# Two transformer blocks on one Trainium2 core: another ordering model, loose ends dealt among products, gate rows in one pass

## The chip, the cores and the metric

The kernel runs on one core of one Trainium2 chip, as one program. The metric is the time of one execution on the device in microseconds. The kernel before has a median of 2524.74 us over three runs (2521.05 to 2525.29).

## The reference, cut to what matters

A sequence of 512 tokens of width 1024 goes through two blocks, all in float32.

```python
# first block
h = rms_norm(x, norm1_g); proj = h @ w_in                # q, k, v and three conv branches
y_attn = chunked_relpos_attention(q, k, v, ...)          # 16 heads, chunks of 64, relative bias
y_conv = bg * conv_w3(cg * xc)                           # gated short convolution
gates = sigmoid(h @ w_gate + b_gate)                     # two branches
x = x + (g_attn * (y_attn @ w_attn_proj) + g_conv * (y_conv @ w_conv_proj)) @ w_out
h2 = rms_norm(x, norm2_g)
x = x + square(relu(h2 @ w_up)) @ w_down                 # 1024 -> 4096 -> 1024
# second block
mod = silu(c) @ w_ada + b_ada                            # six shift, scale and gate vectors
h = rms_norm(x, g_norm1) * (1 + scale1) + shift1
proj = h @ w_in_2
y_sb = stick_breaking(q_sb, k_sb, v_sb)                  # 8 heads of 64, normalised after
y_ml = mlstm(q_ml, k_ml, v_ml, i_pre, f_pre)             # 4 heads of 128; i and f are 4 columns each
x = x + gate1 * (concat(y_sb, y_ml) @ w_out)
h2 = rms_norm(x, g_norm2) * (1 + scale2) + shift2
x = x + gate2 * peer(h2)       # 8 heads: top 16 of 128 x 128 keys, 16384 experts of one row each
```

In `mlstm` the forget gates are summed over time (`A`), the input gates less `A` get a running maximum (`grow`), and each head needs its row of these over all 128 partitions.

## The kernel before, in words

Activations lie transposed, as eight tiles of 128 features x 512 tokens. A value is kept as two parts in a reduced format of float32 that TensorE takes in one pass: a rounded high part and the rest as a low part. A product of weights and activations is three such passes (`mm3`, lines 152 to 156): high by high, high by low, low by high. A weight tile of 1 MB (256 output columns) is loaded by SP into `wraw`, cast on ScalarE into `whi` (line 143) and subtracted on VectorE into `wlo` (line 145), with two buffers of each. `linear` (line 158) makes one 128-row output of 24 passes, `linear2` (line 166) two at once.

**Order.** The program is written as one stream. At the end the framework sets the order of each engine's instructions: it runs the program on a simulated machine and, at each step, gives an engine the earliest instruction of the stream that is ready in that run. The orders are then fixed; on the chip the engines run them in sequence and wait on semaphores. Two simulated machines are to be had; the kernel before uses the default. DMAs are issued in such an order too, nearly all on SP's queue. Tiles come from pools that are opened and closed like a stack, on the left or right side of the memory; a tile that gets memory which another had waits for the last reader of that one.

**First block (`block1`, line 264).** While the inputs load, nine products of ones run (line 285). SP loads the eight x tiles, ScalarE issues the first weight tile in eight pieces of 128 KB (line 289), then makes gain tiles (x times the norm's gain, high and low, `gain_tile`, line 224) and weight halves piece by piece. The gain tiles (pool `hp1`, 32 KB of each partition) are the inputs of all products up to the end of attention, but the pool stays open to the end of the merge. The merge stage makes gates, the attention projection and the output product (lines 403 to 409); behind each of its eight outputs the residual is added and its squares are summed. Then pool `hp2` is opened and all eight gain tiles of the second norm are made (`gain_split`, line 414) before the up product.

**Second block's mixer (`mix`, line 665).** `stick_breaking` (line 821) has two groups of four heads. A head is a generator of seven steps: three of scores, three of shares (cumulative sums by products with a triangle, an exponential, high and low parts) and one that weighs the values. Steps of a head and of the head before it are interleaved ("nonoono", line 913), which leaves four steps of the last head over. At the start of the second group these four run behind the four products that make its queries and keys (lines 899 to 903); at the end four run alone (line 917). `mlstm_in` (line 921) is a generator of the products that feed the mLSTM, each with a short convolution on VectorE and a store; fourteen of its steps follow after `gates` (line 766). `gates` makes the i and f rows by one `linear` whose weight tile has the four i columns at 0 and the four f columns at 32, then their scans, and returns `grow` and `frow` as 4 x 512 tiles of full float32. In `mlstm` (lines 978 and 1020) a product with a selector of ones (`sel`, 4 x 128 for each head) spreads one row over 128 partitions, twice for each head.

**Peer (`peer`, line 1040).** Keys are scored and ranked on VectorE, while products of the first expert weights run ahead (`ahead`). Then one-hot products spread the chosen gates (`spread`), and the experts follow: 128 groups of 128 experts, with weights streamed at 1 MB a tile, while the last 128 tokens are done by gathering rows.

Of the kernel before, what the change touches and what calls it, by code (L numbers as in the profile page):

```python
# [8 lines left out]
F32 = mybir.dt.float32  # L9
F32R = mybir.dt.float32r  # L10
# [11 lines left out]
P = 128  # L22
D = 1024
T = 512
KO = D // P
# [17 lines left out]
V_N1, V_N2, V_GN1, V_GN2 = 0, 8, 16, 24  # L43
# [5 lines left out]
C_ID, C_BONE, C_TRI, C_SBM, C_MLM, C_IOTA, C_SEL, C_ROW = 0, 128, 256, 384, 768, 896, 1024, 1536  # L49
# [20 lines left out]
class Ker:  # L70
# [193 lines left out]
    def block1(self, es_x):  # L264
        from contextlib import ExitStack
        nc, I = self.nc, self.I
# [3 lines left out]
        with ExitStack() as es:  # L270
            hp = es.enter_context(self.pool("hp1", bufs=KO))
            yp = es.enter_context(self.pool("yp1", bufs=KO))
            sp = es.enter_context(self.pool("sp1"))
# [6 lines left out]
            with self.pool("n1") as tp:  # L280
                x0, hs = [], []
                raw, hi, lo = self.weight_tiles()
                pt = self.psum("c", 1)
                for _ in range(9):
                    nc.tensor.matmul(pt[:, :P], self.ones, self.ones, start=True, stop=True)
                for k in range(KO):
                    xt = tp.tile([P, T], F32, name=f"x0_{k}")
                    nc.sync.dma_start(xt, I["x"][k])
                    nc.scalar.dma_start(raw[:, k, :], I["w_in"][16][:, k, :])
                    x0.append(xt)  # L290
                    if k == 0:
                        nc.sync.dma_start(*self.fixed[0])
                nc.sync.dma_start(*self.fixed[1])
                for k, xt in enumerate(x0):
                    hs.append(self.gain_tile(hp, xt, self.v(V_N1 + k), "h1", KO))
                    nc.scalar.copy(hi[:, k, :], raw[:, k, :])  # L296
                    nc.vector.tensor_sub(lo[:, k, :], raw[:, k, :], hi[:, k, :].bitcast(F32))
                nc.vector.tensor_scalar_mul(bgh, self.v(V_BG, 16), 0.5)
                pcs = self.linear2((hi, lo), hs)
                pxs = self.linear2(self.weights(I["w_in"][20]), hs)  # L300
                acc = None
                for k in range(KO):
                    acc = self.sum_sq(tp, acc, x0[k])
                self.rsqrt(tp, self.col_sums(acc), 1.0 / D, out=rstd)
                nc.vector.tensor_mul(rstd2, rstd, rstd)
                pt = self.psum("c", 1)
                for i in range(4):
                    nc.tensor.transpose(pt[:, i * P:(i + 1) * P], rstd[:, i * P:(i + 1) * P], self.ident)
                nc.vector.tensor_copy(rtok, pt.rearrange("p (a b) -> p a b", b=P)[:, :, 0])


            with self.pool("cv", bufs=2) as tp, self.pool("cva") as sp:
                ada = self.ada(sp, range(8))
                ycs = []
                for g in range(4):
# [9 lines left out]
                    for j in range(2):  # L325
                        n = 2 * g + j
# [38 lines left out]
            with self.banks(a=3, b=2, c=2, d=1) as self.ps:  # L365
                ya = self.attention(hs, yp, rstd, rtok, g_dram)

            es_b = es_x.enter_context(ExitStack())
            self.ps = es_b.enter_context(self.banks(a=8))
            with self.pool("mg", bufs=2) as tp, self.pool("mgy", bufs=KO) as mp:  # L370
# [22 lines left out]
                xs = []  # L393
# [4 lines left out]
                for k in range(KO):  # L398
                    xt = xp.tile([P, T], F32, name=f"x{k}")
                    nc.sync.dma_start(xt, I["x"][k])  # L400
                    xs.append(xt)
                acc = None
                for g in range(4):
                    w = self.weights(I["w_out"][g])
                    for j in range(2):
                        n = 2 * g + j
                        po = self.linear(w, j, ms)
                        nc.vector.tensor_add(xs[n], po, xs[n])
                        acc = self.sum_sq(nq, acc, xs[n])
        self.xs = xs  # L410
        self.hp2 = ExitStack()
        hp = self.hp2.enter_context(self.pool("hp2", bufs=KO, side="right"))
        with self.pool("up", bufs=KO + 4) as up, self.pool("mlt", bufs=2) as tp, self.pool("mls") as sp:
            hs = self.gain_split(hp, xs, V_N2, "h2", KO)
            rstd = sp.tile([P, T], F32, name="rstd2")
# [249 lines left out]
    def mix(self, es_x):  # L665
# [21 lines left out]
        with ExitStack() as es:  # L687
# [4 lines left out]
            nc.sync.dma_start(self.mlc, I["consts"][:, C_MLM:C_MLM + P])  # L692
            self.sel = sp.tile([4, 4 * P], F32, name="sel")
            nc.sync.dma_start(self.sel, I["consts"][0:4, C_SEL:C_SEL + 4 * P])
            with self.pool("ci") as tp:
                ci = tp.tile([P, 4 * P], F32, name="ci")
                nc.sync.dma_start(ci, I["consts"][:, C_TRI:C_TRI + 4 * P])
                nc.scalar.copy(cr[:, P:2 * P], ci[:, 0:P])
                nc.scalar.copy(cr[:, 3 * P:6 * P], ci[:, P:4 * P])
            nc.scalar.copy(cr[:, 0:P], self.ident)  # L700
            nc.vector.tensor_scalar_mul(cr[:, 2 * P:3 * P], self.ones, -1.0)
# [6 lines left out]
            steps = lambda n: [next(ml_in, None) for _ in range(n)]  # L708
            mixed = self.stick_breaking(mp, hs, q0, pk)
            rows = self.gates(sp, hs)  # L710
            steps(14)
            es_b.close()
# [53 lines left out]
    def gates(self, sp, hs):  # L766

        nc, I = self.nc, self.I
        with self.pool("gt") as tp:
            raw = tp.tile([P, KO, P], F32, name="if_w")  # L770
            nc.sync.dma_start(raw, I["w_if"])
            hi = tp.tile([P, KO, P], F32R, name="if_h")
            lo = tp.tile([P, KO, P], F32R, name="if_l")
            nc.scalar.copy(hi, raw)
            nc.vector.tensor_sub(lo, raw, hi.bitcast(F32))
            ps = self.linear((hi, lo), 0, hs, tag="b")
            z = tp.tile([P, T], F32, name="if_z")
            nc.scalar.activation(z[:36], ps[:36], AF.Identity, bias=self.v(V_GB)[:36])
            f = tp.tile([4, T], F32, name="if_f")
            nc.vector.tensor_copy(f, z[32:36])  # L780
# [11 lines left out]
            nc.vector.tensor_sub(b, z[0:4], A)  # L792
            grow = sp.tile([4, T], F32, name="grow")
            nc.vector.tensor_tensor_scan(grow, one, b, 0.0, op0=ALU.mult, op1=ALU.max)
            frow = sp.tile([4, T], F32, name="frow")
            nc.vector.tensor_add(frow, A, grow)
# [6 lines left out]
            nc.vector.tensor_copy(bt, pb[:, :16])  # L803
        return bt, grow, frow

# [14 lines left out]

    def stick_breaking(self, mp, hs, pq, pk):
        nc, I = self.nc, self.I
        widths = [512, 384, 256, 256]
        out = []
        with self.pool("sb") as tp, self.pool("sbq", bufs=2) as qp, self.pool("sbv", bufs=4) as vp:
# [70 lines left out]
            for g in range(2):  # L896
                if g:
                    pq, pk = [], []
                    for p, at in ((pq, 0), (pk, 2)):
                        w = self.weights(I["w_in_2"][at + g])  # L900
                        p += [self.qk_in(tp, self.linear(w, j, hs), None) for j in range(2)]
                    for _ in old:
                        pass
                    old = None
                else:
                    pk = [self.qk_in(tp, p, None) for p in pk]
# [3 lines left out]
                for j in range(2):  # L910
                    for f in range(2):
# [4 lines left out]
                        old = new  # L916
            for _ in old:
                pass
        return out
# [638 lines left out]
```

## Time and profile before

| | us |
|---|---|
| median of three runs | 2524.74 |
| the profiled execution | 2522.37 |
| its span, first to last instruction | 2520.6 |
| TensorE busy | 2467.9 (98%) |
| VectorE busy | 1872.7 (74%) |
| ScalarE busy | 1056.6 (42%) |
| GpSimd busy | 624.1 (25%) |
| DMA | 515.03 MB, 204 GB/s over the span |

The profile is of one execution. Busy time counts work, not issuing or waiting; of TensorE the ends of products are modelled. A wait is given to the one that ended it last. The granted clock is a share of the full 2.4 GHz.

### The profile page before, as it was taken

How to read it: one execution, taken by the hardware profiler on the slowest of the kernel's cores; microseconds unless marked ns; L12 is line 12 of the kernel's file. 1: busy time of each engine (PE TensorE's matmuls, PEld its weight loads, DVE VectorE, ACT ScalarE, POOL GpSimd, SP SyncE). 2: the span in 40 equal slices, each digit the busy share in tenths (PEclk: the TensorE clock that was granted, in tenths of full speed). 3: DMA queues.
4: the chain of work that ended last, by engine and by line, in shares of the span. 5: the costliest groups of instructions: out<-in, count | busy, mean ns of one | idle time of the engine just before them, and what ended most of it. 6: DMA issues, size and time to landing. Idle time of an engine off the chain costs nothing.

```text
span 2520.6 us, 33112 instructions
## 1 busy us (share of the span) xinstructions
PE 2467.9 (98%) x12655; PEld 2114.4 (84%) x12655; DVE 1872.7 (74%) x3094; ACT 1056.6 (42%) x1480; POOL 624.1 (25%) x506
## 2 busy tenths in 40 slices
PE   9999999999999999999999989999999999999999
PEld 7887887877888887777789988978889999999998
DVE  5558777855555557897779999857668787888887
ACT  5226555643222236766653345543333333333332
POOL 0001100111011001001035630011135555555552
PEclk9999999999999999999999999999999999999999
DMA  5352323443444332114343357799879999999995
GB/s 202 127 199 99 104 93 101 139 170 135 174 150 148 138 137 85 38 67 138 120 162 120 124 184 276 311 319 341 300 267 333 327 339 333 328 336 335 336 340 195
DMA packets 172312, 515.03 MB, mean 204 GB/s; under 512 B 13396, under 2 KB 78308, under 8 KB 146296
## 3 DMA queue, kind: packets, MB, share of 16 engines
q1 hardware_dynamic: 133960, 376.52, 42.6%
q0 software_dynamic: 37040, 135.35, 14.9%
q8 instruction: 99, 1.62, 0.2%
q10 hardware_dynamic: 1152, 1.05, 0.1%
q14 instruction: 61, 0.50, 0.1%
HBM read 461.47 MB, written 51.38 MB: 203 GB/s over the span
## 4 chain that ended last, share of the span: by engine, by line
PE 76%; DVE 15%; ACT 4%; DMA 2%; issue 2%; SPq 0%; POOL 0%; ACTq 0%; DVEq 0%; POOLq 0%
PE pa L154 12%; PE pa L156 12%; PE pa L155 12%; PE pp L1443 7%; PE pp L1442 7%; PE pp L1446 7%; PE pu L154 4%; PE pu L156 4%; PE pu L155 4%; DVE wlo L145 1%; ACT whi L143 1%; DVE tk_rest L1194 1%; PE pb L596 1%; DVE tk_e L1230 1%; DMA mg_a<-g_dram 1%
## 5 line engine op out<-in xcount | busy, mean ns | idle before, releaser
L143 ACT CAST whi<-wraw 128x2048 fp32r<-128x2048 f32 x229 | 437.6, 1911 | 540.6 <-PE pa L155 296.5
L145 DVE TENSOR_TENSOR wlo<-wraw,whi 128x2048 fp32r<-128x2048 f32 x210 | 489.0, 2329 | 125.7 <-ACT whi L143 119.3
L154 PE MATMUL pa<-hh,whi 128*128 128x512 f32 (+1 forms) x1360 | 523.0, 385 | 7.1 <-ACT whi L296 3.4
L156 PE MATMUL pa<-hh,wlo 128*128 128x512 f32 (+1 forms) x1360 | 516.4, 381 | 2.3 <-DVE wlo L145 2.2
L155 PE MATMUL pa<-lh,whi 128*128 128x512 f32 (+1 forms) x1360 | 518.4, 381 | 0.0
L1443 PE MATMUL pp<-wlo,hew 128*128 128x512 f32 x768 | 299.0, 390 | 1.5 <-DVE wlo L145 1.5
L1442 PE MATMUL pp<-whi,hew 128*128 128x512 f32 x768 | 298.7, 390 | 1.7 <-ACT hew L1409 1.1
L1152 POOL DMA_INDIRECT r_row<-in_u_rows,r_at x128 | 184.4, 1440 | 461.7 <-DVE r_w L1173 419.6
L154 PEld LDWEIGHTS pa<-hh,whi 128*128 128x128 f32 x1360 | 257.6, 190 | 47.0 <-ACT whi L296 3.6
L156 PEld LDWEIGHTS pa<-hh,wlo 128*128 128x128 f32 x1360 | 257.2, 189 | 44.6 <-issue 3.6
L155 PEld LDWEIGHTS pa<-lh,whi 128*128 128x128 f32 x1360 | 257.5, 189 | 40.9 <-issue 5.3
L1446 PE MATMUL pp<-whi,lew 128*128 128x512 f32 x768 | 237.1, 389 | 0.0
L1152 POOL DMA_INDIRECT r_row<-in_expert_v,r_at x128 | 194.0, 1516 | 173.2 <-DVE r_big L1181 135.7
L156 PE MATMUL pu<-hh,wlo 128*128 128x384 f32 x640 | 215.0, 336 | 0.0
L154 PE MATMUL pu<-hh,whi 128*128 128x384 f32 x640 | 215.0, 336 | 0.0
L155 PE MATMUL pu<-lh,whi 128*128 128x384 f32 x640 | 214.9, 336 | 0.0
L1446 PEld LDWEIGHTS pp<-whi,lew 128*128 128x128 f32 x768 | 144.1, 188 | 30.3
L1443 PEld LDWEIGHTS pp<-wlo,hew 128*128 128x128 f32 x768 | 144.1, 188 | 29.6 <-DVE wlo L145 2.3
L1442 PEld LDWEIGHTS pp<-whi,hew 128*128 128x128 f32 x768 | 144.1, 188 | 29.2 <-ACT hew L1409 1.3
L1181 DVE SCALAR_TENSOR_TENSOR r_big<-r_row,r_w,r_big 128x1024 f32<-128x1024 f32 x127 | 162.9, 1283 | 3.0
L1409 ACT CAST hew<-ex_w 128x384 fp32r<-128x384 f32 x128 | 65.5, 513 | 226.3 <-DVE ex_w L1405 149.1
L1173 DVE CUSTOM_DVE_ANT_0 r_row<-r_row,r_big 128x1024 f32<-128x1024 f32 x128 | 151.3, 1220 | 0.0
(440 smaller groups left out, 4480.1 us busy)
## 6 DMA issues: line engine op xcount, KB each, us to landing
wraw<-in_expert_u SPq DMA_DIRECT2D x64, 1024.0 KB, 7.4
wraw<-in_expert_v SPq DMA_DIRECT2D x64, 1024.0 KB, 7.6
wraw<-in_w_in SPq DMA_DIRECT2D x37, 1024.0 KB, 4.9
ada_w<-in_w_ada SPq DMA_DIRECT2D x24, 1024.0 KB, 4.8
gate_dram<-oh_s SPq DMA_DIRECT2D x12, 2048.0 KB, 7.0
ex_g<-gate_dram SPq DMA_DIRECT2D x31, 768.0 KB, 10.9
wraw<-in_w_up SPq DMA_DIRECT2D x16, 1024.0 KB, 5.3
wraw<-in_w_down SPq DMA_DIRECT2D x16, 1024.0 KB, 4.8
```

What stands on the lines that cost most here:

```text
L143: nc.scalar.copy(hi, raw)
L145: nc.vector.tensor_sub(lo, raw, hi.bitcast(F32))
L154: mm(out, wh, xh, start=start, stop=False)
L155: mm(out, wh, xl, start=False, stop=False)
L156: return mm(out, wl, xh, start=False, stop=stop)
L1152: self.nc.gpsimd.indirect_dma_start(t, None, src, at)
L1173: later(nc.vector.tensor_tensor_reduce(row, row, h, 1.0, 0.0, op0=ALU.mult, op1=ALU.add, accum_out=w[:, k:k + 1]))
L1181: later(nc.vector.scalar_tensor_tensor(acc, row, w[:, k:k + 1], acc, op0=ALU.mult, op1=ALU.add))
L1409: nc.scalar.copy(hi, w)
L1442: mm(sums[b][half], hi, v[0][:, c, hc], start=n == 0, stop=False)
L1443: mm(sums[b][half], hi, v[1][:, c, hc], start=False, stop=False)
L1446: mm(sums[b][half], lo, v[0][:, c, hc], start=False, stop=n == P - 1)
```

## The change

- The framework orders the instructions by its other simulated machine (the flag on `TileContext`).
- The first weight tile is issued by ScalarE in three pieces (one, three and four input tiles) behind the loop over x.
- `hp1` lies on the right side and is closed after attention; `hp2` is opened within the merge, and each gain tile is made behind its output product.
- The selector is a tile of 36 rows in the reduced format, with ones in rows 0 to 3 and 32 to 35.
- `gates` puts the low half of its weights into columns 64 to 127 of the high half's tile, so two passes for each input tile give high and low rows apart, and adds them. It returns `grow` and `frow` as 36 rows in the reduced format, high parts in rows 0 to 3 and low parts in rows 32 to 35.
- One left-over step of the last head runs behind each of the four query and key products, and two steps of `mlstm_in` run between the left-over steps at the end; twelve follow after `gates` instead of fourteen.

```diff
@@ block1
-            hp = es.enter_context(self.pool("hp1", bufs=KO))
+            es_h = ExitStack()
+            hp = es_h.enter_context(self.pool("hp1", bufs=KO, side="right"))
...
                     nc.sync.dma_start(xt, I["x"][k])
-                    nc.scalar.dma_start(raw[:, k, :], I["w_in"][16][:, k, :])
                     x0.append(xt)
                     if k == 0:
                         nc.sync.dma_start(*self.fixed[0])
+                for a, b in ((0, 1), (1, 4), (4, KO)):
+                    nc.scalar.dma_start(raw[:, a:b, :], I["w_in"][16][:, a:b, :])
...
                 ya = self.attention(hs, yp, rstd, rtok, g_dram)
+            es_h.close()
...
-                acc = None
+                self.hp2 = ExitStack()
+                hp = self.hp2.enter_context(self.pool("hp2", bufs=KO, side="right"))
+                acc, hs = None, []
...
                         nc.vector.tensor_add(xs[n], po, xs[n])
                         acc = self.sum_sq(nq, acc, xs[n])
+                        hs.append(self.gain_tile(hp, xs[n], self.v(V_N2 + n), "h2", KO))
         self.xs = xs
-        self.hp2 = ExitStack()
-        hp = self.hp2.enter_context(self.pool("hp2", bufs=KO, side="right"))
...
-            hs = self.gain_split(hp, xs, V_N2, "h2", KO)
@@ mix
-            self.sel = sp.tile([4, 4 * P], F32, name="sel")
-            nc.sync.dma_start(self.sel, I["consts"][0:4, C_SEL:C_SEL + 4 * P])
+            self.sel = sp.tile([36, 4 * P], F32R, name="sel")
...
+                cs = tp.tile([36, 4 * P], F32, name="cs")
+                nc.vector.memset(cs, 0.0)
+                for p in (0, 32):
+                    nc.sync.dma_start(cs[p:p + 4], I["consts"][0:4, C_SEL:C_SEL + 4 * P])
+                nc.scalar.copy(self.sel, cs)
...
-            mixed = self.stick_breaking(mp, hs, q0, pk)
+            mixed = self.stick_breaking(mp, hs, q0, pk, steps)
             rows = self.gates(sp, hs)
-            steps(14)
+            steps(12)
@@ gates
-            hi = tp.tile([P, KO, P], F32R, name="if_h")
-            lo = tp.tile([P, KO, P], F32R, name="if_l")
-            nc.scalar.copy(hi, raw)
-            nc.vector.tensor_sub(lo, raw, hi.bitcast(F32))
-            ps = self.linear((hi, lo), 0, hs, tag="b")
+            w = tp.tile([P, KO, P], F32R, name="if_h")
+            nc.scalar.copy(w[:, :, :64], raw[:, :, :64])
+            nc.vector.tensor_sub(w[:, :, 64:], raw[:, :, :64], w[:, :, :64].bitcast(F32))
+            ps = self.psum("b")
+            for k in range(KO):
+                for i in range(2):
+                    nc.tensor.matmul(ps, w[:, k, :], hs[k][i], start=k + i == 0, stop=k + i == KO)
             z = tp.tile([P, T], F32, name="if_z")
             nc.scalar.activation(z[:36], ps[:36], AF.Identity, bias=self.v(V_GB)[:36])
+            nc.vector.tensor_add(z[:36], ps[64:100], z[:36])
...
-            grow = sp.tile([4, T], F32, name="grow")
+            grow = tp.tile([4, T], F32, name="if_g")
...
-            frow = sp.tile([4, T], F32, name="frow")
+            frow = tp.tile([4, T], F32, name="if_r")
...
-        return bt, grow, frow
+            out = []
+            for n, x in (("g", grow), ("f", frow)):
+                both = sp.tile([36, T], F32R, name=f"{n}row")
+                nc.gpsimd.memset(both.bitcast(F32), 0.0)
+                nc.scalar.copy(both[0:4], x)
+                nc.vector.tensor_sub(both[32:36], x, both[0:4].bitcast(F32))
+                out.append(both)
+        return bt, *out
@@ stick_breaking
-                        p += [self.qk_in(tp, self.linear(w, j, hs), None) for j in range(2)]
-                    for _ in old:
-                        pass
+                        for j in range(2):
+                            p.append(self.qk_in(tp, self.linear(w, j, hs), None))
+                            next(old)
...
-            for _ in old:
-                pass
+            for i, _ in enumerate(old):
+                if i % 2:
+                    steps(1)
@@ kernel
-    with tile.TileContext(nc) as tc:
+    with tile.TileContext(nc, schedule_with_timeline_sim=True) as tc:
```

## Rows read from the trace of the kernel before

**Rows 1.** The page: span, and busy time of each engine (share, instructions).

```profile
span 2520.6 us, 33112 instructions
...
PE 2467.9 (98%) x12655; PEld 2114.4 (84%) x12655; DVE 1872.7 (74%) x3094; ACT 1056.6 (42%) x1480; POOL 624.1 (25%) x506
```

**Rows 2.** The page: the chain that ended last, by engine.

```profile
PE 76%; DVE 15%; ACT 4%; DMA 2%; issue 2%; SPq 0%; POOL 0%; ACTq 0%; DVEq 0%; POOLq 0%
```

**Rows 3.** By stretch: length, busy PE PEld DVE ACT POOL, clock, DMA share, GB/s.

```profile
630.00:693.00 63.00, 63.00 (x278) 51.95 (x277) 32.77 (x41) 13.35 (x9) 4.37 (x4) 1.00 0.48 175
1008.00:1071.00 63.00, 57.52 (x314) 47.76 (x313) 53.55 (x90) 45.09 (x79) 4.75 (x6) 0.97 0.11 38
1071.00:1134.00 63.00, 59.11 (x293) 48.89 (x292) 59.00 (x102) 43.77 (x79) 4.29 (x8) 0.97 0.19 66
...
1449.00:1512.00 63.00, 56.20 (x356) 54.59 (x355) 60.01 (x218) 26.44 (x35) 24.49 (x18) 0.95 0.52 186
1953.00:2016.00 63.00, 63.00 (x322) 57.40 (x321) 50.13 (x65) 21.01 (x23) 33.33 (x23) 1.00 0.92 328
```

**Rows 4.** Waits of TensorE: line, waited for, us in total, times, longest.

```profile
PE pb L1319 <- DVE pk_i L1236: 6.8, 1, 6.8
PE pd L550 <- DVE sb_wh L871: 5.7, 2, 3.4
...
PE pa L154 <- ACT whi L296: 3.4, 1, 3.4
PE pa L154 <- ACT hh L229: 2.9, 1, 2.9
PE pa L156 <- DVE wlo L145: 2.2, 1, 2.2
```

**Rows 5.** By stretch, as in rows 3: four stretches at half clock.

```profile
588.73:592.14 3.41, 3.40 (x5) 1.83 (x6) 3.41 (x5) 3.41 (x6) 0.00 (x0) 0.50 0.31 74
1042.72:1046.13 3.41, 3.22 (x10) 2.69 (x11) 1.67 (x4) 0.92 (x3) 0.00 (x0) 0.50 0.00 0
1124.64:1128.05 3.41, 2.90 (x9) 2.65 (x10) 2.58 (x2) 0.60 (x2) 0.02 (x1) 0.50 0.21 77
1486.43:1493.26 6.83, 5.33 (x17) 5.23 (x18) 6.73 (x11) 0.17 (x1) 4.19 (x2) 0.50 0.18 25
```

**Rows 6.** Instructions by time, 0 to 20 us: start, us, engine, line, tiles.

```profile
4.63 2.84 ACTq L289 DMA_DIRECT2D wraw<-in_w_in  x5
4.83 0.17 DVE L298 TENSOR_SCALAR bgh<-vec 128x16 f32<-128x16 f32 x1 [3.83 <-DMA vec<-in_vecs]
...
7.52 0.72 ACT L229 ACTIVATE hh<-x,vec 128x512 fp32r<-128x512 f32 x1 [4.85 <-DMA wraw<-in_w_in]
...
8.59 1.22 PE L154 MATMUL pa<-hh,whi 128*128 128x512 f32 x2 [3.36 <-ACT whi L296]
...
18.22 2.29 DVE L145 TENSOR_TENSOR wlo<-wraw,whi 128x2048 fp32r<-128x2048 f32 x1 [1.87 <-ACT whi L143]
```

**Rows 7.** Instructions by time, ScalarE and VectorE, 585 to 588 us.

```profile
585.64 1.90 ACT L143 CAST whi<-wraw 128x2048 fp32r<-128x2048 f32 x1 [3.95 <-PE pa L155]
585.87 0.69 DVE L408 TENSOR_TENSOR x<-pa,x 128x512 f32<-128x512 f32 x1 [3.45 <-PE pa L156]
...
587.98 5.00 ACT L229 ACTIVATE hh<-x,vec 128x512 fp32r<-128x512 f32 x8
```

**Rows 8.** The chain of waits in order of time: start, us, what.

```profile
1180.37 1.07 PE pg L978 x2
...
1224.99 1.05 PE pd L1020 x2
```

**Rows 9.** Instructions by time: a scan of the gates, the first row product.

```profile
1161.85 1.20 DVE L794 TENSOR_TENSOR_SCAN grow<-if,if_b 4x512 f32<-4x512 f32 x1
...
1165.27 1.12 PE L978 MATMUL pg<-grow,sel 4*128 4x512 f32 x2
```

**Rows 10.** The page: DMA issues, KB each, us to landing.

```profile
wraw<-in_expert_v SPq DMA_DIRECT2D x64, 1024.0 KB, 7.6
```

More of the change, by code (lines that the diff above doesn't have):

```diff
@@ L819, in head_norm, with stick_breaking @@
         return self.split(mp, t, "mx", KO // 2)
-    def stick_breaking(self, mp, hs, pq, pk):
+    def stick_breaking(self, mp, hs, pq, pk, steps):
         nc, I = self.nc, self.I
```

## The prediction

> **What bounds the kernel now.** I read the page's busy times first [rows 1]: TensorE is busy 2467.9 of 2520.6 us, so all that can be won without taking products away is 52.7 us of idle time, plus what runs at the lower clock level. VectorE stands at 74%. The chain of waits [rows 2] gives 76% of the span to TensorE and 15% to VectorE: the reader is to see that VectorE, not DMA, ends most of what TensorE waits for. The table by stage comes next [rows 3]. In a dense stretch (630 to 693 us) 278 products of 512 columns fill 63.00 us, 0.227 us each at the full clock; that is my price of one product. In the stick-breaking stage (1008 to 1134 us) TensorE has 57.52 and 59.11 of 63 us and VectorE 53.55 and 59.00, so there VectorE is nearly full. Before the experts (1449 to 1512) TensorE has 56.20. In the expert stage (1953 to 2016) TensorE is full and the DMA engines stand at 0.92. Last the waits of TensorE by releaser [rows 4], which put names to the holes, and the stretches at half clock behind the larger ones [rows 5]: granted clock 0.50, the level of 1.2 GHz, after the engine had been idle. TensorE busy 3.40, 3.22 and 2.90 us at half speed is 1.7, 1.6 and 1.45 us of work lost.
>
> **The change part by part.** The sum is made against the profiled run, 2522.37 us with its span of 2520.6 and 1.8 us around it. The median, 2524.74, is 2.4 us above that run; I carry that over.
>
> *Start.* ScalarE issues eight weight pieces itself. Its last five issues run from 4.63 to 7.47 us, and the first gain tile starts at 7.52, right behind them, although VectorE could use the vectors at 4.83 [rows 6]. The first product follows 1.07 us later, at 8.59, and its wait is the 3.4 us in [rows 4]. With three issues in place of eight, ScalarE is free before its data is there: the gain tile can start near 4.9, the product near 5.9, at most 2.7 us earlier. What is late next is the second weight tile: its low half is made from 18.22 to 20.51 us [rows 6], while the first 48 products end no sooner than 8.59 + 48 x 0.227 = 19.5. If that load doesn't move, nothing is won. Ends 0 and 2.7. I take 2.0, nearer the upper row, since five fewer DMAs stand in the two queues ahead of that load.
> The Trainium skill speaks against that (DMA: Bandwidth & Descriptors, section "Issuing engines are not separate DMA queues"): DMAs started on several engines share the same 16 DMA engines, and starting them otherwise saves only the starter's own time. By it the second weight tile lands when it landed, this term is near 0 and the sum 18.7. No run here tells yet whether that load is held by its place in the queue or by the bytes ahead of it.
>
> *From the output product to the up product.* The second gain tiles now get the memory that the first block's inputs leave after attention, and each is made behind its own product. Before, all eight are made in one run on ScalarE from 587.98 (5.00 us), after a weight cast at 585.64 that stands ahead of them and after the last product's sum at 585.87 [rows 7]; TensorE waits 2.9 us for the first [rows 4] and loses 1.7 at half clock [rows 5]: 4.6. After, tile 7 alone is late: 585.87 + 0.69 for the sum, 0.63 on ScalarE, about 0.7 on VectorE, some 588. TensorE, starting at 585.8, needs it after 42 products, 9.5 us on. The seven moved tiles are ScalarE and VectorE work of some 0.63 and 0.7 us beside products of 24 x 0.227 = 5.4 us each; a weight cast queued behind one is late by 0.63 at most. The x loads now wait for the gate products to finish with that memory, on SP's queue among the gate loads, but no instruction reads them before the first output product. Ends 2.9 (the clock still falls for another reason) and 4.6; I take 4.6, as no wait is left to start it.
>
> *Gate rows in one pass.* A product of the selector with a gate row takes two instructions and 1.07 or 1.05 us [rows 8]; there are eight of them (two for each of four heads). In the reduced format each is one pass over 512 columns, at 0.227 [rows 3]. 8 x (1.05 - 0.227) = 6.6. No trace of before shows 36 rows in this format; a pass of 128 rows costs 0.227, so I give 6.0 and 6.6 as ends and take 6.6. All stand in TensorE's own stream.
> The Trainium skill (FP8 and Floating Point Precision, section "TensorE Precision Notes") has full fp32 as four passes through the array. By that a row product would be 4 x 0.227 = 0.91, the gain 5.5 and the sum 1.1 smaller; the row shows 1.05, so the row is used.
>
> *Gate product.* For each of eight input tiles three products become two, both halves of the weights side by side in one: 24 to 16, 8 x 0.227 = 1.8 gone. Added are one VectorE add of 36 rows on the chain, and behind each scan a ScalarE copy and a VectorE subtraction (0.6 to 0.7 each by the neighbours in [rows 7]), with two GpSimd memsets beside them. The scan ends at 1163.05 and the first row product starts at 1165.27 [rows 9], so 2.2 us of slack meet 2.0 of new chain while TensorE arrives 1.8 earlier: up to 1.6 of new wait for what is queued there, the first head. Ends a loss of 1.0 and a gain of 1.8; I take a gain of 0.8. The new selector (a memset, two small loads, one copy) lies in a stage with room.
>
> *Loose ends of stick-breaking.* The last head of the first group was finished behind four products; now one of its steps goes behind each, so its shares and values come some three products (16 us) earlier in the order. The hole behind it is one of the two waits of 5.7 in [rows 4], 3.4 us, with 1.6 at half clock: 5.0. The second is 2.3 with 1.45: 3.8; there two of the fourteen steps of the next stage's inputs are moved between the last head's steps, each with its weight load, 24 products, one ScalarE copy, four VectorE passes and a store on SP's queue, ahead of the gate weights' load. What stands against both gains is that VectorE has 59.00 of 63 us of work [rows 3] and none is taken away. Ends 0 and 8.8; I take 3.8 and 2.9, three quarters, since while TensorE stood in the holes VectorE was working on this very chain, and the deal starts that chain sooner.
>
> *Ordering model.* Every engine's order is set at build time by a simulated run; the flag swaps the machine in it. No row shows the new order. On the good side it can reach the waits that no edit touches: 6.8 for the first transposes before the experts and 2.2 for a low half [rows 4], and 5.33 us of half-clock work [rows 5], 2.7: 11.7 together. On the bad side nothing in the trace bounds it short of the rivals below. I take 0.
>
> Sum: 2.0 + 4.6 + 6.6 + 0.8 + 3.8 + 2.9 = 20.7. From the profiled run 2501.7; on the median 2524.74 - 20.7 = 2504. Low ends: 0 + 2.9 + 6.0 - 1.0 + 0 = 7.9, so 2517; high ends: 2.7 + 4.6 + 6.6 + 1.8 + 8.8 = 24.5, so 2500.
>
> **The rivals.**
> *B, the order wins too.* The 11.7 us come on top: 2504 - 12 = 2492. For it: TensorE has other products to run in front of those transposes. Against: VectorE is at 60.01 of 63 there [rows 3], and the pieces dealt into that stage are counted by hand.
> *C, VectorE holds the stick-breaking stage.* The deal and the start give nothing, as VectorE's 59.00 of 63 has no room: 2524.74 - (4.6 + 6.6 + 0.8) = 2513.
> *D, the other side: late expert weights.* In the expert stage TensorE is full, the DMA engines carry 328 GB/s at a share of 0.92 [rows 3], and 64 tiles land 7.6 us after their issue [rows 10]. If the new order sets tile loads behind gather, gate or row traffic so that tiles come late by a landing, each costs up to 7.6 us. It decides from four such tiles on (30 us against 20.7); five give 2504 + 38 = 2542. Against it: in that stage no TensorE wait is large now.
> *E, the change doesn't do what it says.* The old order already pulled ready work forward, and the new one loses elsewhere what the shorter rows save: 2525.
>
> **How the numbers follow.** My forecast of 2504 (own range 2498 to 2510) has 0.42; B 0.17; C 0.17; E 0.09; D 0.15. A measurement of this kernel can tell 0.2%, 5 us, from no change. Faster: 0.42 + 0.17 + 0.17 = 0.76; same: E, 0.09; slower: D, 0.15. The range 2484 to 2531 leaves out the low tail of B (0.04) and nearly all of D (0.14).
>
> **What would show it.** After: the first product near 6 us; no wait of TensorE for a gain tile and no half clock at the up product; the row products one instruction each, near 0.23; 16 products at the gate weights; no wait over 1 us for the shares' weights. The expert stage should show TensorE at 63 of 63. I am wrong if TensorE's idle time rises in stages that no edit touches, and the whole forecast fails if the expert stage grows by more than 20 us.

## The result, and the profile after

The changed kernel takes 2591.99 us (median of four runs, 2589.95 to 2595.92) against 2524.04 us for the kernel before on the same chip: ratio 1.0273, 95% interval 1.0258 to 1.0288. The forecast was 2504 us. Its profiled execution took 2595.92 us, 73.5 us of span more than before [rows 1]. First the page: span, busy time, the clock in 40 slices, the chain by engine.

```profile
span 2594.1 us, 33089 instructions
...
PE 2488.0 (96%) x12639; PEld 2139.6 (82%) x12639; DVE 1871.5 (72%) x3098; ACT 1064.8 (41%) x1483; POOL 637.2 (25%) x508
...
PEclk9999999899999999997999999989999999999999
...
PE 82%; DVE 12%; ACT 3%; issue 1%; DMA 1%; POOL 0%; SPq 0%; DVEq 0%; ACTq 0%; POOLq 0%
```

VectorE, ScalarE and GpSimd have the work they had. TensorE has 16 instructions less and is busy 20.1 us more, and idle 106.1 us (span less busy) against 52.7. More idle time and more busy time together are the sign of half clock: products after a hole take twice as long. Next four of the stretches of [rows 3] in the changed kernel, and the one behind the second of the mixer's: length, busy PE PEld DVE ACT POOL, clock, DMA share, GB/s.

```profile
630.00:693.00 63.00, 63.00 (x278) 52.00 (x277) 37.96 (x43) 15.31 (x15) 10.11 (x8) 1.00 0.42 150
1008.00:1071.00 63.00, 56.66 (x318) 48.15 (x316) 53.13 (x89) 45.40 (x80) 6.81 (x9) 0.99 0.15 51
1071.00:1134.00 63.00, 61.02 (x283) 50.03 (x284) 48.61 (x66) 36.16 (x57) 8.54 (x12) 0.95 0.25 84
1134.00:1197.00 63.00, 48.05 (x277) 41.08 (x276) 49.21 (x84) 36.13 (x62) 0.33 (x2) 0.89 0.37 130
1953.00:2016.00 63.00, 63.00 (x320) 57.22 (x319) 50.01 (x65) 22.88 (x24) 33.82 (x23) 1.00 0.94 332
```

The dense stretch and the expert stage are full, as before. The loss is in three other places, the ends of three stages whose steps go back and forth between TensorE and VectorE: the end of attention, of stick-breaking, and of the one-hot products. The first row is of the kernel before, the other three of the changed one.

```profile
480.00:520.00 40.00, 40.00 (x188) 32.96 (x187) 23.13 (x35) 20.02 (x28) 6.36 (x6) 1.00 0.75 257
```

```profile
480.00:520.00 40.00, 28.01 (x115) 21.05 (x113) 32.41 (x97) 24.82 (x59) 6.93 (x12) 0.80 0.49 171
1134.00:1213.00 79.00, 55.29 (x301) 46.78 (x301) 55.93 (x95) 39.56 (x68) 0.33 (x2) 0.85 0.30 105
1680.00:1725.00 45.00, 26.38 (x275) 22.00 (x274) 27.21 (x24) 18.93 (x35) 0.00 (x0) 0.78 0.68 262
```

TensorE is idle 12.0, 23.7 and 18.6 us there, 54.3 together, and the clock falls to 0.78 to 0.85. Between the same products of both kernels: from the first score of attention to the first merge product it is idle 22.6 us against 4.4 before, from the first score of stick-breaking to the gates' transposes 32.0 against 11.3, from the first one-hot product to the rows of x 17.6 against 3.4. That is 53.1 of the 53.4 us by which idle time grew. A fourth place, from the mixer's output product to the first product of the keys, grew from 1.8 to 13.6, and stretches with less idle time than before make up for it. The waits by releaser answer to [rows 4]: line, waited for, us in total, times, longest.

```profile
PE pd L553 <- DVE sb_y L557: 10.0, 2, 6.8
PE pu L1125 <- DMA xc<-x_dram: 9.8, 4, 9.2
PE pb L785 <- DVE if_h L781: 7.5, 1, 7.5
PE pb L811 <- DVE if_b L802: 6.7, 1, 6.7
PE pd L553 <- DVE at_y L557: 6.2, 6, 2.2
PE pb L599 <- DVE at_st L601: 5.6, 3, 3.4
PE pa L154 <- ACT hmx L181: 5.4, 1, 5.4
PE pb L1337 <- DVE pk_i L1254: 4.6, 1, 4.6
```

The last was 6.8 before [rows 4]; of the others none was over 1.0 us at a time. Of the steps here an edit touches those of `if_h` and `if_b` and what stands beside the last stick-breaking steps (`sb_y`); but in the run with the flag alone, below, TensorE has all of these waits too: 6.7 us for `if_h`, 5.9 for `if_b`, 10.3 for `sb_y`, 9.8 for `xc`. In the orders of the two programs, 62 products of the block's inputs stand between attention's last score product and the first merge product before the change, and none after; between the last one-hot product and the rows of x it is 94 and none.

### The profile page after: what moved, and what is told of

Same layout as the page of the kernel before. It is cut to its first block, busy times and chain, and to the rows that moved or that the text cites. A ratio compares the mean times of both kernels' runs of the same rounds, so it can differ in the third digit from the quotient of the medians.

```text
span 2594.1 us, 33089 instructions
## 1 busy us (share of the span) xinstructions
PE 2488.0 (96%) x12639; PEld 2139.6 (82%) x12639; DVE 1871.5 (72%) x3098; ACT 1064.8 (41%) x1483; POOL 637.2 (25%) x508
## 4 chain that ended last, share of the span: by engine, by line
PE 82%; DVE 12%; ACT 3%; issue 1%; DMA 1%; POOL 0%; SPq 0%; DVEq 0%; ACTq 0%; POOLq 0%
PE pa L154 14%; PE pa L156 14%; PE pa L155 14%; PE pp L1461 7%; PE pp L1464 7%; PE pp L1460 7%; PE pu L154 4%; PE pu L156 4%; PE pu L155 4%; DVE tk_rest L1212 1%; PE pb L599 1%; PE pd L513 1%; PE pd L553 1%; PE pd L554 1%; DVE tk_i L1210 1%
## 5 line engine op out<-in xcount | busy, mean ns | idle before, releaser
L1170 POOL DMA_INDIRECT r_row<-in_expert_v,r_at x128 | 206.7, 1615 | 161.7 <-DVE r_big L1199 132.4
```

The source lines that it names most:

```text
L1170: self.nc.gpsimd.indirect_dma_start(t, None, src, at)
```

## The experiments

The reference of each run is the kernel before on the same chip, 2522.4 to 2524.5 us.

### Flag and edits apart

The flag alone on the kernel before (`e1_flag_only`):

```
-    with tile.TileContext(nc) as tc:
+    with tile.TileContext(nc, schedule_with_timeline_sim=True) as tc:
```

> The kernel before, with the other ordering model and no other edit. Theory O (the new order costs all of it, the edits save about 20): 2524 + 68 + 20 = about 2610, with new TensorE idle time in attention, in the stick-breaking stage and in the spread stage. Rival F (the edits cost it, the order is neutral): within 12 us of 2524. Rival M (attention and spread, which no edit touches and which shifted by about 24 and 15 us, belong to the order; the mixer's 30 us to the dealt steps and the gates): 2524 + 39 = about 2563.

2605.95 us, +83.5 (ratio 1.0334, interval 1.0316 to 1.0351). Then all else of the change without that line:

> All the edits with the default ordering model. Theory O: 2504 as the prediction's sum had it (2498 to 2510). Rival F: 2580 or more. Rival M: the mixer's 30 us stay, less some 14 for the gain tiles, the start and the rows: about 2540.

2516.18 us, -6.3 (0.9972, 0.9963 to 0.9982). So the flag costs all of the loss and more; the edits save 6 us in the first order and some 15 in the other one (1.0334 against 1.0273), where 20.7 were forecast. The edits in parts: the weight pieces at the start with the gain tiles behind their products,

> The kernel before with two edits alone, default ordering: three weight pieces in place of eight at the start, and the first block's inputs on the right side with the gain tiles made behind each output product. Theory O, by the prediction's terms: 2.0 + 4.6 = 6.6 saved, 2517, no TensorE wait for a gain tile and no half clock at the up product. Rivals F and M say the same of these two edits, unless the moved pool is what disturbs attention: then attention grows here too, by up to 24 us.

2520.29 us, -2.2 (0.9987, 0.9978 to 0.9997); the shorter gate rows and gate product,

> The kernel before with the gate edits alone, default ordering: selector and gate rows of 36 rows in the reduced format, gate weights with both halves side by side. Theory O, by the prediction's terms: 6.6 + 0.8 saved, about 2517. Rival M: the longer chain behind the gate product is what opens the two holes of 7.5 and 6.7 us there, so 2525 to 2535.

2520.71 us, -1.7 (0.9992, 0.9982 to 1.0001), which the interval doesn't tell from nothing; and the dealing of the loose ends,

> The kernel before with only the loose ends of stick-breaking dealt among other products (two halves of the middle, every second step of the end). Forecast for this term 6.7 us: 2518 us. By what the other edits left of the sum: 2522.5 us. Rival C (VectorE holds this stage): 2524 us within 1.5, with the waits of 3.4 and 2.4 us for sb_wh still there.

2523.31 us, +0.5 (1.0003, 0.9994 to 1.0012), nothing, with the two waits of [rows 4] still there:

```profile
PE pd L550 <- DVE sb_wh L871: 5.7, 2, 3.4
```

The run is no test of the dealing, though: in its trace every engine has the same instructions in the same order as in the kernel before (told apart by operation, tiles and form). The steps were moved in the stream, and the planner, which takes what is ready, put them where they had been.

### Are bare ends the cause?

First the effect by hand in the kernel before: attention's four gate products per group are written ahead of the group's heads, not behind them (`e8_gates_ahead`).

```
+ for n2 in (2 * g, 2 * g + 1):          # the gate products
+     ...
  for j in range(2):                     # the heads
      ...
- for n2 in (2 * g, 2 * g + 1):
-     ...
```

> The other way about: the kernel before with its own ordering model and only one thing moved in the program, attention's gate products ahead of the four heads of their group. Theory C: the last group's heads are then without products beside them in the first order too, and the time goes up by what the other model lost there, 2522 + 23 = 2545 us (2537 to 2552), with TensorE idle and half clock near 480 to 520 us. Theory T: 2522 us within 5, since the planner and the other engines are as before.

2557.67 us, +34.6 (1.0130, 1.0113 to 1.0147): more than forecast, since three groups, not the last alone, now have a 4 us wait at their value products. So taking the products early does cost tens of us, with the other engines planned anew around them. The other way, in the other ordering model, products were held back behind the chain's steps: the gates in attention, then mixer products too, then the expert steps among the one-hots as well (this one on the changed kernel).

```
+ if self.hold is not None:              # in mm3
+     self.behind(first, self.hold)
  ...
+ self.hold = marks[2 * (n2 - 2 * g) + j]   # last score product of a head
  pg = self.linear(gw, j, hs)
```

> The kernel before with the other ordering model, and with each of attention's four gate products per group tied behind the last score product of one head, where the first order has them. Theory C (cover spent early): the other model has TensorE do ready products ahead of the products that wait for a chain on VectorE and ScalarE, so the chain's last links stand bare. Milestones put 23 us of the 83 us at the end of attention, so 2606 - 23 = 2583 us (2576 to 2590), and the bare row of 16 score products near 485 us is gone. Theory T (the other engines' orders make the chains longer, TensorE's order is not the cause): 2606 us, within 6.

> The same with the mixer's products held as well: of the 14 that the planner has done before the last stick-breaking head ends, five are tied behind that head's last score product and four behind its last value product. Theory C: another 25 of the 33 us that the milestones put between 1000 and 1210 us, 2583 - 25 = 2558 us (2545 to 2570), with fewer than 8 us of TensorE idle between the last head and the gates' transposes where there are 27. Theory T: above 2595 us.

> The changed kernel with its ordering model kept, both holds, and a third: in the spread stage each expert step is tied behind the one-hot product before it, and the 16 kept for the end behind the last one. Theory C: 2592 - 23 - 28 - 18 = 2523 us (2508 to 2540), so that most of the ordering model's loss is these three places. Theory T: above 2575 us. In between, 2545 to 2570: the three places are half of it and the rest is spread thin.

2638.36, 2641.41 and 2642.64 us: +115 to +120, each worse than the flag alone, where 2583, 2558 and 2523 were expected. The theory that three bare ends are all of it falls. The holes didn't close, they moved: from the first to the last score of attention TensorE is idle 48.2 us in `e6_flag_gates_held`, 16.5 with the flag alone and 4.4 before. Its longest waits there are at the start of each group:

```profile
PE pb L600 <- DVE at_st L602: 15.5, 4, 5.1
PE pb L600 <- POOL ka L526: 11.9, 3, 4.6
PE pd L514 <- ACT qn_s L512: 10.2, 3, 3.4
```

### Whose order?

The orders differ on every engine. Counted as the instructions outside the longest sequence that both orders have in common: 1712 of TensorE's 12534 products, 881 of 2758 on VectorE, 321 of 1424 on ScalarE, 94 of 573 on SP's queue, 14 of 509 on GpSimd. So whole engines were tied into one of the two orders, each instruction behind the one that precedes it there, with no wait added on the engine itself.

```
+ for a, b in zip(order, order[1:]):     # one engine's order, written into the kernel
+     tc.add_manual_dep(keep[b].ins, keep[a].ins.name, NoSync, reason="order")
```

The engines left free are planned anew around the tied one, by the machine that the kernel uses. TensorE in the first order under the other machine; and TensorE in the other order in the kernel before, under the first:

> The kernel before with the other ordering model, but every one of its 12534 TensorE products tied behind the product that stands before it in the first order; only the orders of the other engines and queues are the other model's. Theory P (what costs the 83 us is TensorE's order): 2522 us within 8. Theory T (VectorE, ScalarE or the DMA queues are ordered worse, TensorE only waits for them): 2580 us or more. Between, 2535 to 2575, both.

> The cross of it: the kernel before with its own ordering model, and TensorE's 12534 products tied into the order that the other model made in the run with the flag alone. Theory P: 2606 us within 10, with the bare tails at the end of attention, of stick-breaking and of the one-hots. Theory T: below 2545 us.

2588.66 us (+64.3; 1.0261, 1.0244 to 1.0277) and 2620.70 us (+96.3; 1.0387, 1.0372 to 1.0403). TensorE's order is not the cause by itself: with the good one 64 us stay. Nor does either run change TensorE's order alone, as the expectations have it. By the traces VectorE's order in the first of them differs from that with the flag alone in 482 of 3094 instructions and from the first order in 747; in the second it differs from the first order in 388. Here is what it waits for then. VectorE by time at the first head of attention, in `e12_flag_first_pe_order`, and below it the kernel before: start, us, line, tiles.

```profile
227.71 0.28 DVE L598 CUSTOM_DVE_ANT_0 at_e<-pb,bias 128x128 f32<-128x128 f32 x1
...
229.10 2.29 DVE L145 TENSOR_TENSOR wlo<-wraw,whi 128x2048 fp32r<-128x2048 f32 x1 [1.11 <-ACT whi L143]
231.31 0.42 DVE L598 CUSTOM_DVE_ANT_0 at_e<-pb,bias 128x256 f32<-128x256 f32 x1
```

```profile
228.05 0.28 DVE L598 CUSTOM_DVE_ANT_0 at_e<-pb,bias 128x128 f32<-128x128 f32 x1
...
228.26 0.42 DVE L598 CUSTOM_DVE_ANT_0 at_e<-pb,bias 128x256 f32<-128x256 f32 x1
...
230.56 2.28 DVE L145 TENSOR_TENSOR wlo<-wraw,whi 128x2048 fp32r<-128x2048 f32 x1
```

In the kernel before all four scores of a head are taken off before the weight's low half is made. In `e12_flag_first_pe_order` the low half stands between the first and the second score (with the flag alone it stands ahead of both); its high half isn't there yet, VectorE sits 1.11 us, works 2.29, and TensorE, which needs the score's bank, waits (products have the line of the tie's helper in this kernel):

```profile
231.79 0.50 PE L1548 MATMUL pb<-ka,qa 128*128 128x512 f32 x1 [3.04 <-DVE at_st L598]
```

The Trainium skill (TensorE: Matmul & The Clock Gate, section "Architectural detail: the array is 16x 32x32, not 1x 128x128") has VectorE and ScalarE as strict first in, first out; these rows agree: 0.42 us of work that could have run at 228 stood 3 us behind one that could not.

The ladder from there: VectorE tied as well, or ScalarE, or both, and at last all five.

> The other ordering model with TensorE and VectorE both tied into the first order; ScalarE, GpSimd and the load queues are left to it. Theory V (VectorE's order is what the pinned TensorE waited for: weight splits that wait for their high half stand ahead of the short steps that release TensorE): the 64 us of the run with TensorE alone tied go, 2522 to 2535 us. Theory A (ScalarE's order) or Q (the loads): 2575 us or more.

> The same with TensorE and ScalarE tied, VectorE left to the other model. Theory V: 2575 us or more, as with TensorE alone tied (2589). Theory A: 2522 to 2540 us.

> TensorE, VectorE and ScalarE tied into the first order, so that only the load queues and GpSimd are the other model's. Theory V or A: 2522 us within 6. Theory Q: 2555 us or more.

> The control of the ties: the other ordering model with all five engines and queues tied into the first order. If ties cost nothing and the rest was the load queue (the keys' load waited for, 5.4 us at 1305.6 us): 2524 us within 3. If ties cost something by themselves: 2530 to 2536 us, as with three tied.

| in the first order | us | over before | ratio, interval |
|---|---|---|---|
| none (flag alone) | 2605.95 | 83.5 | 1.0334 (1.0316 to 1.0351) |
| TensorE | 2588.66 | 64.3 | 1.0261 (1.0244 to 1.0277) |
| TensorE, VectorE | 2568.14 | 43.7 | 1.0175 (1.0158 to 1.0192) |
| TensorE, ScalarE | 2565.24 | 40.8 | 1.0167 (1.0150 to 1.0184) |
| these three | 2535.75 | 11.3 | 1.0046 (1.0031 to 1.0061) |
| all five | 2523.19 | 0.4 | 1.0001 (0.9992 to 1.0010) |

No single engine carries it; theories V and A are each half right, and the load queue and GpSimd have the last 11 us. As the free engines are planned anew in each row, the steps between rows are no shares of 83.5 us that belong to one engine. With three tied, 5.5 us of the 11 are lost at the keys, whose load GpSimd issues at 1303.48 us where it was 1295.27; another 4.6 stand in the expert stage. The wait at the keys:

```profile
PE pb L1548 <- DMA keys<-in_sub_keys: 5.4, 1, 5.4
```

All five tied gives the time before, so the ties themselves cost nothing and the flag acts through the orders alone. The cross of the ladder, VectorE tied into the other order under the first machine:

> The kernel before with its own ordering model, VectorE alone tied into the order that the other model made; TensorE is free to be planned around it. Theory V: 2570 us or more. Theory A or Q: 2522 to 2545 us.

2666.36 us, +141.9 (1.0563, 1.0546 to 1.0581): worse than all engines in it together. VectorE's order is that of the flag here, but TensorE's is a third one: 1436 of its 12655 instructions lie outside what it has in common with the first order, 1245 with the flag's. So an order is good or bad with the orders of its partners; what VectorE's costs by itself no run shows.

### Two repairs of the edits

`e10_edits_x_held` is all edits in the first order, with the loads of x tied behind the merge's last gate load; `e11_rows_128` adds zeros, so that the gate rows fill 128 partitions.

```
- nc.sync.dma_start(xt, I["x"][k])
+ self.behind(nc.sync.dma_start(xt, I["x"][k]), load.ins.name)
...
- self.sel = sp.tile([36, 4 * P], F32R, name="sel")
+ self.sel = sp.tile([P, 4 * P], F32R, name="sel")
```

> All edits without the other model (2516.2 us before), and the eight loads of x tied behind the last gate load of the merge on the load queue. If the wait of TensorE for hm at 544 us (2.8 us and a half-clock stretch of 6.8 us, where 2.9 and 3.4 stood at the up product before) comes from these loads standing between the merge's loads: that wait goes and 2516 - 4 = 2512 us. If it comes from VectorE's extra gain tiles: 2516 us within 1.5, with the wait still there.

> The same, with the selector and the two gate rows on 128 partitions, zeros below row 36. If a product's 0.43 us comes from its short stationary tile (36 rows): 0.23 us for each of the eight, 1.6 us less than the run beside it. If it comes from where it stands (a switch of tiles, a wait): the same time and the same 0.43 us.

2514.27 us (0.9959, 0.9946 to 0.9973) and 2510.46 us (0.9945, 0.9931 to 0.9958). Both beat the kernel before and the changed one. The wait for `hm` is down to 0.5 and 0.4 us. The row product shrinks as forecast, but that this gives time isn't shown: from the first row product to the first transposes of the peer stage the two traces have 132.2 and 132.3 us, and the 3.8 us between the medians are near the runs' spreads (2510.86 to 2514.43 and 2508.83 to 2511.92).

## Why the prediction was wrong

**The step that failed** is the ordering model: "On the bad side nothing in the trace bounds it short of the rivals below. I take 0." It costs 83.5 us, four times the whole sum. Its own range had a good side of 11.7 and no bad side, although the rule it was told by, an order fixed at build time from a simulated run, meant that every engine's order was open. What the runs showed in place of the 0: the orders together cost 83.5 us (the flag alone), and nothing is left of it when all five are put back (2523.19 us). The stage rows held a warning, if no bound: between the dense stretch and the experts VectorE has 53 to 60 of 63 us [rows 3], so how products lie among its steps matters (moving one set of them, in attention, cost 34.6 us in `e8_gates_ahead`). Rival E had this mechanism in a clause ("the new one loses elsewhere") and priced it at what the shorter rows save; rival D, the slower side, looked for it in the expert stage, which didn't change: 859.1 us from its first product to its last before, 858.9 after. "TensorE's idle time rises in stages that no edit touches" is the sign that came true.

**Start**, 2.0 forecast. In `e2_edits_only` the first product comes 1.5 us earlier, at 7.09 us, and not at 5.9: the gain tile waits for the load of the vectors, which the text took as there at 4.83 [rows 6].

```profile
6.02 0.72 ACT L229 ACTIVATE hh<-x,vec 128x512 fp32r<-128x512 f32 x1 [3.35 <-DMA vec<-in_vecs]
```

The limit named next, the second weight tile, is not what TensorE waited for: it has no wait there in either trace. And the lead doesn't last. It is 1.2 us at 38 us and 0.3 at 143 us, since the products that read the moved gain tiles start 0.2289 us apart where it was 0.2267, at the full clock. In 80 us that is 351 products instead of 354 (first `e2_edits_only`, then the kernel before):

```profile
60.00:140.00 80.00, 80.00 (x351) 65.63 (x350) 44.67 (x47) 20.86 (x18) 7.94 (x10) 1.00 0.37 130
60.00:140.00 80.00, 80.00 (x354) 66.24 (x354) 44.88 (x48) 20.89 (x18) 7.94 (x10) 1.00 0.37 131
```

All six kernels with the moved pool have 351 or 352 there, all fourteen without it 354 or 355; why isn't shown. No term of the sum had this.

**From the output product to the up product**, 4.6 forecast. The wait for the gain tile went, as said, but one that stood 41 us earlier, at the output product's own inputs, grew. Waits of TensorE in `e3_start_and_gain`, and below it in the kernel before:

```profile
PE pa L154 <- ACT hm L393: 3.2, 1, 3.2
```

```profile
PE pa L154 <- ACT hm L390: 0.9, 1, 0.9
```

and the half clock behind it, in the edited kernel alone:

```profile
547.40:554.20 6.80, 6.42 (x15) 4.55 (x16) 3.65 (x4) 1.24 (x2) 0.00 (x0) 0.50 0.46 157
```

2.3 us more of wait and 3.2 at half clock are lost; 2.9 + 1.7 are won, and 0.6 of the wait for the low parts there. From the first output product to the first down product it is 97.4 us against 97.7, so 0.3 is left of the term. The sentence that failed: the x loads wait "among the gate loads, but no instruction reads them before the first output product". That is true of the loads, not of what stands behind them on SP's queue. Of eight issues, four go out at 511 and 519 us in front of the merge's own loads; before, all were out by 496.7. The merge's last load goes out at 537.76 instead of 534.95. First the edited kernel, then the kernel before:

```profile
496.83 1.34 SPq L403 DMA_DIRECT2D x<-in_x  x3
...
511.11 0.90 SPq L403 DMA_DIRECT2D x<-in_x  x2
513.99 0.33 SPq L384 DMA_DIRECT2D mg_a<-g_dram  x1
...
519.17 0.90 SPq L403 DMA_DIRECT2D x<-in_x  x2
```

```profile
489.36 4.76 SPq L400 DMA_DIRECT2D x<-in_x  x7
```

Holding those loads took the wait away, and the same stretch takes 92.5 us in `e10_edits_x_held`: 5.2 us won, so the term was right but for this wait.

**Gate rows in one pass**, 6.6 forecast. The term was mis-sized and then eaten. A row product of 36 rows takes 0.43 us from its start to the next, not 0.227 (the first of the eight 0.98, as the next product isn't ready), so the stream of `e4_rows` has 4.0 us of them where it had 8.5: 4.5 won. In `e10_edits_x_held`, and with 128 rows in `e11_rows_128`:

```profile
1182.31 0.28 PE L156 MATMUL pn<-ml_wh,lmv 128*128 128x256 f32 x1
1182.52 0.50 PE L1038 MATMUL pd<-frow,sel 36*128 36x512 f32 x1
1182.95 0.44 PE L156 MATMUL ps<-hq,lk 128*128 128x384 f32 x1
```

```profile
1182.84 0.28 PE L156 MATMUL pn<-ml_wh,lmv 128*128 128x256 f32 x1
1182.96 0.40 PE L1038 MATMUL pd<-frow,sel 128*128 128x512 f32 x1
1183.19 0.34 PE L156 MATMUL ps<-hq,lk 128*128 128x384 f32 x1
```

But from the first row product to the first transposes of the peer stage the time is 134.7 us before and 135.0 in `e4_rows`: TensorE came earlier to the keys' low parts and waits 1.7 us for them, 0.7 before, and the execution has two stretches at half clock in it.

```profile
PE ps L156 <- POOL lk L182: 1.7, 2, 1.2
```

```profile
1173.40:1176.80 3.40, 3.27 (x13) 3.17 (x14) 2.16 (x4) 1.04 (x3) 0.08 (x1) 0.50 0.66 243
1272.40:1275.80 3.40, 3.40 (x7) 1.74 (x6) 1.80 (x3) 2.08 (x2) 0.00 (x0) 0.50 1.03 352
```

That the wait brings these stretches isn't shown: in `e10_edits_x_held` the wait is the same 1.7 us, neither stretch follows, and the time is 132.2 us, 2.5 won; and `e5_deal_only`, with the instructions of the kernel before, has the second of them too.

**Gate product**, 0.8 forecast: 2.7 in `e4_rows`, by the time from the last value product of stick-breaking to the gates' transposes (33.9 us before, 31.2 after). That is above the term's own upper end of 1.8; where the rest comes from is open.

**Loose ends**, 6.7 forecast, three quarters of the bound: nothing. The step that failed is "so its shares and values come some three products (16 us) earlier in the order": in `e5_deal_only` no instruction changed its place. Rival E's clause "The old order already pulled ready work forward" is what happened here. Rival C had the time right but not the reason: whether VectorE, at 59.00 of 63 us [rows 3], would have held a real deal back was not tried.

## What to carry to other kernels

Where a planner fixes in-order queues, its choice is a change to every engine at once, and it can cost more than all hand edits together: run it alone before anything is built on it, and forecast it with a bad side of its own. A step moved in the source isn't moved on the engine: read the order from the trace before a run is taken as a test of it. A product moved early is not free: ask which chain it was covering. A load that nothing needs yet still delays what is queued behind it.

## What the runs showed of the hardware

- A product of a short stationary tile between full ones isn't as cheap as its columns: 36 rows took 0.43 us, 128 rows with zeros 0.23, and the product ahead of it 0.21 instead of 0.12: 0.3 us for each. The Trainium skill (TensorE: Matmul & The Clock Gate, section "Why this matters for your kernels") has a product of 32 rows take as long as one of 128; here, among products of 128 rows, it took longer, and why was not tried.
- Products on the first gain tiles stand 0.2289 us apart instead of 0.2267, at the full clock, in the six kernels that moved their pool; that the place of the tiles does it isn't shown.
- Ties that only fix the order on one engine cost nothing that can be measured: 2523.19 us with all engines tied (`e21_flag_all_first`), 2522.82 without.
- Holes cost twice: the flag's 81 us of span are 59 us more idle time and 22 us more busy time for the same products, at a mean granted clock of 0.979 against 0.995.

Open: why the other machine orders so (which durations it takes was not looked at), which engine's order costs what, and why VectorE in its order with TensorE planned anew costs more than the whole of it.
